# The opening of a two-layer trunk on one core: norm weights packed with the first chunk of x, first weights on a second DMA queue, first products in another order

## The chip, the cores and the metric

The kernel runs on one core of a Trainium2 chip. A core has a matrix engine (TensorE, PE in the profile, with the loading of its weights as PEld), VectorE (DVE), ScalarE (ACT), GpSimd (POOL) and SyncE (SP), which only issues transfers. Each engine takes its own instructions in order; they wait for each other through semaphores. Transfers are issued by an engine into its queue and carried out by 16 DMA engines. The metric is the device time of one execution in microseconds (us); three runs of a kernel are taken, and their median counts.

## The reference

x is one sequence of 512 tokens by 1024 features. Two layers each add an attention block and an MLP to it; everything is float32.

```python
for l in range(DEPTH):                                   # DEPTH = 2
    h = rmsnorm(x, attn_norm[l])
    proj = jnp.einsum('bsd,de->bse', h, w_in[l])         # 1024 -> 3072
    sb_q, sb_k, sb_v, df_q, df_k, df_v = jnp.split(proj, splits, axis=-1)
    sb_out = stick_breaking_attention(sb_q, sb_k, sb_v)
    ...
    dq = rope(df_q, pos)
    dk = rope(df_k, pos)
    df_heads = differential_attention(dq, dk, dvv, lam)
    df_out = rmsnorm(df_heads, subln_norm[l]) * (1.0 - lambda_init)
    mixed = jnp.concatenate([sb_out, df_out], axis=-1)
    x = x + jnp.einsum('bse,ed->bsd', mixed, w_o[l])
    h = rmsnorm(x, mlp_norm[l])
    u = jnp.square(jax.nn.relu(jnp.einsum('bsd,df->bsf', h, w_ff1[l])))
    x = x + jnp.einsum('bsf,fd->bsd', u, w_ff2[l])
return rmsnorm(x, final_norm)

def rmsnorm(x, g):
    return x * lax.rsqrt(jnp.mean(x * x, axis=-1, keepdims=True) + EPS) * g
```

## The kernel before

**Products.** x lies in SBUF with features on the 128 partitions, as 8 chunks of 128x512. Every float32 operand is split into a rounded high part and the rest (`_hi`, `_lo`), and a product of two operands is done as three matmuls, hi·hi, hi·lo and lo·hi, into one PSUM bank (`three`, lines 293 to 298). A block of 128 output features over all of x is thus 8 chunks times 3, 24 matmuls of 128x512, which the text calls products. The weights of such a block are one unit of 128x1024; `_Weights` loads it into one of three raw buffers (`raw`, line 112), splits it (line 130 on ACT for the high part, line 131 on DVE for the rest) and loads the next one into the buffer that this frees. High and low parts go into `whi` and `wlo`; some units early in the program have another home, the tiles `mdh`, `mdl` (later used for mixed heads) and `vs`.

**The norm.** The first norm is folded in late. The gain is multiplied into x when h is made (`make_h`, h_hi on ACT at line 247, h_lo on DVE at line 248), so the first products need no norm. Its other factor, one number for each token, comes from the sum of squares: ACT squares each chunk (line 256), DVE adds them into `ssq` (line 257), TensorE transposes the sum (`rms_a`, line 277, bank rs_a), DVE reduces it to `ms`, POOL takes the power into `rcol`, TensorE transposes that back (`rms_b`, line 290, bank rb_a), ACT copies it into ssq (line 291), and DVE multiplies it into the tables of cosine and sine, `cs` (lines 778 and 779). The first banks are emptied by multiplications with cs (`u0d0q`, `v0d0q`, lines 489 and 490).

**The opening.** Two units, written p in the profile (u0 and u1 in `dense`: the queries and keys of the first pair of differential heads, later evicted as d0q and d0k), run first, then p0d1q, p0d1k (the same for the second pair, from the mdh and mdl tiles), then the wide values v0w, token block by token block. Before them ten warm-up matmuls on zeros occupy TensorE (`WARM`, line 36). x comes in eight transfers of 256 KB on SP's queue, and the two raw tiles of the first units in four pieces of 128 KB each, a pair of pieces ahead of every second chunk of x (lines 211 to 215). The norm weights, 42 columns, come on ACT's queue (line 209), ahead of ACT's table load.

**What sets the order.** The instructions of each engine are ordered when the program is built, by a scheduler with estimated times, from the order in which the code issues them and what they depend on; `behind` ties one instruction behind another on the same engine by hand. `RA` and `RB` (line 37) say after which block step the two transposes are issued in `dense` (lines 774 to 779). Within the opening nothing is tied by hand: the products of a chunk and a unit are issued by `three`, chunk by chunk up to chunk 4, then unit 0 and unit 1 for chunks 5 to 7.

**Further on.** The rotated q and k of a differential pair are moved on chip into other partitions by small transfers of 64x512 on SP (`st0d0k`, `st0d0q`, `kl0d0k`, line 464, from hl0d0k); the first scores, S0d (line 521), are multiplied from st0d0k and st0d0q. SP's queue also carries the weight loads, in program order.

Of the kernel before, what the change touches and what calls it, by code (L numbers as in the profile page):

```python
# [9 lines left out]
F32 = mybir.dt.float32  # L10
# [7 lines left out]
P = 128  # L18
S = 512
# [13 lines left out]
LAG2, LAG3, KSB = 2, 3, 7  # L33
MTB = 1
TB = 4
WARM = 10
RA, RB = (21, 23), (32, 31)
MAN = ()
_CTX = {}
DLY_R, DLY_D, DLY_S = 3.5, 8.0, 6.0  # L40
# [56 lines left out]
class _Weights:  # L97
# [15 lines left out]
            self.raw[i] = t  # L113
            self.loaded += 1

    def split_part(self, i, a, b):
        nc = self.nc
        if i not in self.tiles and i in self.home:
            self.tiles[i] = self.home[i]
        if i not in self.tiles:  # L120
            k = self.spot(i)
            self.owner[k] = i
            self.turn = k + 1
            pool = self.pools[k > 1]
            hi = pool.tile([P, 1024], F32R, tag="whi", name=f"whi{i}")
            lo = pool.tile([P, 1024], F32R, tag="wlo", name=f"wlo{i}")
            self.tiles[i] = (hi, lo)
        hi, lo = self.tiles[i]
        raw = self.raw[i]
        h = nc.scalar.activation(hi[:, a:b], raw[:, a:b], AF.Copy)  # L130
        self.last = h, nc.vector.tensor_tensor(  # L131
            out=lo[:, a:b], in0=raw[:, a:b], in1=hi[:, a:b].bitcast(F32), op=ALU.subtract)
        if _UNITS[i][0] in "fq":
            self.line(*self.last)
        if self.gate and i < self.gate[0]:
            self.gate[2](self.last[1], self.gate[1])
# [35 lines left out]


@with_exitstack
def trunk(ctx, tc, xT, w, w1, w2, gains, gfin, lamv, cos, sin, out):
    nc = tc.nc
    cp = ctx.enter_context(tc.tile_pool(name="cp", bufs=1))
    wraw = ctx.enter_context(tc.tile_pool(name="wraw", bufs=3))
# [14 lines left out]
    if MAN:  # L193
        ctx.enter_context(tc.manual_schedule(engines={getattr(mybir.EngineType, e) for e in MAN}))
    W = _Weights(nc, w, wraw, wspl)
    cp.tile([P, 96], F32, tag="lead", name="lead")
    x = cp.tile([P, KC, S], F32, tag="x", name="x")
    h_hi = cp.tile([P, KC, S], F32R, tag="h_hi", name="h_hi")
    h_lo = cp.tile([P, KC, S], F32R, tag="h_lo", name="h_lo")
    ssq = cp.tile([P, S], F32, tag="ssq", name="ssq")  # L200
# [4 lines left out]
    ident = edge[:, 384:512]  # L205
    lam_sm = cp.tile([P, L, 2], F32, tag="lamsm", name="lam_sm")
    lam_ex = cp.tile([P, L, 2], F32, tag="lamex", name="lam_ex")
    g_all = cp.tile([P, 42], F32, tag="g", name="g_all")
    nc.scalar.dma_start(g_all, gains)
    raws = [wraw.tile([P, 1024], F32, tag="raw", name=f"raw{i}") for i in range(2)]  # L210
    for c in range(KC):
        nc.sync.dma_start(x[:, c, :], xT[c])
        if c % 2 == 0:
            for i in range(2):
                nc.sync.dma_start(raws[i][:, c * P : (c + 2) * P], w[i][:, c * P : (c + 2) * P])
    W.raw = dict(enumerate(raws))
    W.loaded = 2
    W.load(3)
# [12 lines left out]
    def gcol(which, l, c):  # L231
        i = {"attn": l * 8, "mlp": 16 + l * 8, "final": 32, "sub": 40 + l}[which] + c
        return g_all[:, i : i + 1]
# [12 lines left out]
    def make_h(c, g):  # L246
        a = nc.scalar.activation(h_hi[:, c, :], x[:, c, :], AF.Copy, scale=g)
        return a, nc.vector.scalar_tensor_tensor(
            out=h_lo[:, c, :], in0=x[:, c, :], scalar=g, in1=h_hi[:, c, :].bitcast(F32),
            op0=ALU.mult, op1=ALU.subtract)  # L250
# [42 lines left out]
    def three(pt, a, b, first, last, onto=False):  # L293
        ah, al = a
        bh, bl = b
        return (nc.tensor.matmul(pt, ah, bh, start=first, stop=False, skip_group_check=onto),  # L296
                nc.tensor.matmul(pt, ah, bl, start=False, stop=False, skip_group_check=onto),  # L297
                nc.tensor.matmul(pt, al, bh, start=False, stop=last, skip_group_check=onto))  # L298
# [33 lines left out]
    for l in range(L):  # L332
        last = l == L - 1
        with ExitStack() as actx:
# [23 lines left out]
                return a2.tile([P, 2, 2, S], F32R, tag="hl", name=name)  # L358

            if l == 0:  # L360
                for c in range(KC):
                    if c % 2 == 0:
                        for i in range(2):
                            W.split_part(i, c * P, (c + 2) * P)
                    opened = make_h(c, gcol("attn", 0, c))
                W.split = 2
                at_home(2, md_parts)
                at_home(6, vs_parts)
# [384 lines left out]
            def dense():  # L753
                pts = opened_by.pop() if l else None
                if l == 0:
                    us = [W.next("x"), W.next("x")]
                    pts = [bank("mm", f"p{l}{i}") for i in range(2)]
                    turns = [(c, i) for c in range(5) for i in range(2)] + [(c, i) for i in range(2) for c in (5, 6, 7)]
                    for c, i in turns:
                        three(pts[i], wpair(us[i], c), hpair(c), c == 0, c == KC - 1)  # L760
                        yield 3 * 0.216
                step, b = 2 * KC, int(ORDER[0][1])
                held = [(pts[0], "d", b, "q"), (pts[1], "d", b, "k")]
# [432 lines left out]
def _layout(inputs):  # L1196
# [23 lines left out]
    for n, (l, g, q, c) in enumerate(_QUAD):  # L1220
# [6 lines left out]
    xT = np.ascontiguousarray(x.reshape(S, KC, P).transpose(1, 2, 0))  # L1227
    an, mn, fn, sn = (np.asarray(inputs[k]) for k in ("attn_norm", "mlp_norm", "final_norm", "subln_norm"))
    gains = np.concatenate([an.reshape(L * KC, P), mn.reshape(L * KC, P), fn.reshape(KC, P), sn], 0)
    lam = np.stack([np.asarray(inputs[k]) for k in ("lam_q1", "lam_k1", "lam_q2", "lam_k2")], 1)  # L1230
    inv = (1.0 / (np.float32(10000.0) ** (np.arange(0, 64, 2, dtype=np.float32) / np.float32(64)))).astype(np.float32)
    ang = (np.arange(S, dtype=np.float32)[None, :] * inv[:, None]).astype(np.float64)
    cs, sn_ = np.cos(ang).astype(np.float32), np.sin(ang).astype(np.float32)
    return {
        "xT": xT,
        "w": wu,
        "w1": wp.reshape(len(_QUAD), P, 1024),
        "w2": wq.reshape(len(_QUAD), P, 1024),
        "gains": np.ascontiguousarray(gains.T),
        "gfin": np.ascontiguousarray(fn.reshape(D)),  # L1240
        "lamv": np.ascontiguousarray(lam.reshape(-1)),
        "cos": np.concatenate([cs * np.float32(SCALE)] * 2 + [cs] * 2, 0),
# [22 lines left out]
```

## Time and profile before

| | us |
|---|---|
| median of three runs | 1123.84 |
| the three runs | 1123.77, 1123.84, 1124.44 |
| the profiled execution | 1124.27 |
| its span, first to last instruction | 1122.5 |
| mean granted clock of TensorE | 0.998 |

The rows of the profile used below have these forms. A row of the time line has the start in us from the span's begin, the length in us, the engine (a name with q is its queue: issuing instructions), the line of the kernel, the operation, the output and inputs by name with shape, a count where equal instructions are grouped, and in brackets the idle time of the engine just before and what ended it. A row of waits has the engine and its line, what was waited for, the total in us, the number of times and the longest. A row of a window has busy time and number of instructions for each engine, then the clock, the DMA share and GB/s. Matmuls overlap, so a product's own length is longer than the distance to the next one; the distance counts.

### The profile page before, as it was taken

The page shows a single profiled execution, that of the slowest core. Times are in us where ns is not written, and L with a number is a line of the kernel's source. Part 1 is how long each engine was busy: PE and PEld are TensorE (multiplying, and loading weights), DVE is VectorE, ACT ScalarE, POOL GpSimd, SP SyncE. Part 2 cuts the span into 40 slices and gives each one's busy share as a digit, 9 for nine tenths or more (in the row PEclk, how much of TensorE's full clock was granted, in tenths as well). Part 3 has the DMA queues.
Part 4 walks back from the last instruction along what each step waited for, and adds up shares of the span by engine and source line. Part 5 has one row for each costly group of instructions (what it writes and reads, how often), then busy time and mean ns, then how long its engine had stood idle before and what let it go on. Part 6 is the DMA issues. An engine that isn't in the chain of part 4 may idle for free.

```text
span 1122.5 us, 17662 instructions
## 1 busy us (share of the span) xinstructions
PE 1109.8 (99%) x6642; PEld 983.8 (88%) x6642; DVE 925.7 (82%) x1228; ACT 710.4 (63%) x1112; POOL 172.7 (15%) x257
## 2 busy tenths in 40 slices
PE   9999999999999999999999999999999999999997
PEld 6788989889799899899888888888998998998986
DVE  7788778788897877878888787887988888888787
ACT  6455667577867557567555467675777665565675
POOL 1001333210210110201100014341101102011012
PEclk9999999999999999999999999999999999999999
DMA  7647433266887776875646463523578768759665
GB/s 251 190 121 218 114 113 113 75 170 185 184 207 202 175 175 208 185 189 159 125 148 171 111 182 110 153 85 128 118 220 193 188 188 183 194 154 202 170 136 146
DMA packets 60468, 183.36 MB, mean 163 GB/s; under 512 B 7520, under 2 KB 8544, under 8 KB 60384
## 3 DMA queue, kind: packets, MB, share of 16 engines
q1 hardware_dynamic: 46272, 131.62, 36.7%
q0 software_dynamic: 13824, 50.34, 25.4%
q8 instruction: 52, 0.85, 0.3%
q10 hardware_dynamic: 288, 0.28, 0.1%
q14 instruction: 32, 0.26, 0.1%
HBM read 154.95 MB, written 2.10 MB: 140 GB/s over the span
## 4 chain that ended last, share of the span: by engine, by line
PE 78%; DVE 11%; ACT 3%; DMA 3%; issue 3%; POOL 1%; SPq 0%; POOLq 0%; DVEq 0%; ACTq 0%
PE f L298 8%; PE f L296 8%; PE f L297 8%; DVE wlo L131 3%; PE x L297 3%; PE x L298 3%; PE x L296 3%; PE wo L296 2%; PE wo L297 2%; PE wo L298 2%; DMA q<-in_w 1%; ACT whi L130 1%; DVE C0s L539 1%; DVE C1s L539 1%; PE T0s L609 1%
## 5 line engine op out<-in xcount | busy, mean ns | idle before, releaser
L131 DVE TENSOR_TENSOR wlo<-q,whi 128x1024 fp32r<-128x1024 f32 x184 | 223.9, 1220 | 23.2 <-ACT whi L130 22.4
L130 ACT ACTIVATE whi<-q 128x1024 fp32r<-128x1024 f32 x184 | 190.6, 1052 | 56.8 <-DMA q<-in_w 28.0
L296 PE MATMUL f<-T_hi,whi 128*128 128x256 f32 x512 | 145.5, 284 | 0.0
L298 PE MATMUL f<-T_hi,wlo 128*128 128x256 f32 x512 | 144.9, 283 | 0.0
L297 PE MATMUL f<-T_lo,whi 128*128 128x256 f32 x512 | 144.9, 283 | 0.0
L862 POOL DMA_DIRECT2D q<-in_w x64 | 56.3, 914 | 368.5 <-DVE wlo L131 349.0
L296 PE MATMUL f<-h_hi,whi 128*128 128x256 f32 x384 | 108.8, 283 | 0.0
L297 PE MATMUL f<-h_lo,whi 128*128 128x256 f32 x384 | 108.7, 283 | 0.0
L298 PE MATMUL f<-h_hi,wlo 128*128 128x256 f32 x384 | 108.7, 283 | 0.0
L297 PEld LDWEIGHTS f<-T_lo,whi 128*128 128x128 f32 x512 | 98.3, 192 | 0.0
L296 PEld LDWEIGHTS f<-T_hi,whi 128*128 128x128 f32 x512 | 98.3, 192 | 0.0
L298 PEld LDWEIGHTS f<-T_hi,wlo 128*128 128x128 f32 x512 | 98.2, 192 | 0.0
L953 ACT ACTIVATE F<-F 128x512 f32<-128x512 f32 x112 | 70.5, 629 | 21.7 <-DVE F L958 17.8
L130 ACT ACTIVATE whi<-raw 128x1024 fp32r<-128x1024 f32 (+1 forms) x58 | 55.6, 969 | 29.8 <-PE wo L297 7.8
L296 PEld LDWEIGHTS f<-h_hi,whi 128*128 128x128 f32 x384 | 73.7, 192 | 0.4
L297 PEld LDWEIGHTS f<-h_lo,whi 128*128 128x128 f32 x384 | 73.7, 192 | 0.3
L298 PEld LDWEIGHTS f<-h_hi,wlo 128*128 128x128 f32 x384 | 73.7, 192 | 0.1
L131 DVE TENSOR_TENSOR wlo<-raw,whi 128x1024 fp32r<-128x1024 f32 (+1 forms) x58 | 66.3, 1155 | 6.0 <-ACT whi L130 5.8
L243 ACT ACTIVATE Ahx<-F 128x1024 fp32r<-128x1024 f32 x32 | 34.0, 1063 | 55.7 <-PE x L297 24.3
L243 DVE TENSOR_TENSOR Alx<-F,Ahx 128x1024 fp32r<-128x1024 f32 x32 | 39.2, 1225 | 9.0 <-ACT Ahx L243 9.0
L243 DVE TENSOR_TENSOR Al<-F,Ah 128x1024 fp32r<-128x1024 f32 x24 | 29.4, 1224 | 16.5 <-ACT Ah L243 16.5
L243 ACT ACTIVATE Ah<-F 128x1024 fp32r<-128x1024 f32 x24 | 25.4, 1060 | 19.4 <-issue 15.0
(970 smaller groups left out, 3234.3 us busy)
## 6 DMA issues: line engine op xcount, KB each, us to landing
q<-in_w SPq DMA_DIRECT2D x100, 512.0 KB, 4.7
q<-in_w POOLq DMA_DIRECT2D x84, 512.0 KB, 6.8
raw<-in_w SPq DMA_DIRECT2D x62, 512.0 KB, 4.1
yw<-in_w SPq DMA_DIRECT2D x12, 512.0 KB, 5.0
yw<-in_w POOLq DMA_DIRECT2D x12, 512.0 KB, 5.6
cs<-in_w SPq DMA_DIRECT2D x8, 512.0 KB, 6.5
ww<-in_w SPq DMA_DIRECT2D x8, 512.0 KB, 3.9
x<-in_xT SPq DMA_DIRECT2D x8, 256.0 KB, 4.2
```

Source lines behind the costliest of these rows:

```text
L130: h = nc.scalar.activation(hi[:, a:b], raw[:, a:b], AF.Copy)
L131: self.last = h, nc.vector.tensor_tensor(out=lo[:, a:b], in0=raw[:, a:b], in1=hi[:, a:b].bitcast(F32), op=ALU.subtract)
L243: return nc.scalar.activation(hi, src, AF.Copy), nc.vector.tensor_tensor(out=lo, in0=src, in1=hi.bitcast(F32), op=ALU.subtract)
L296: return (nc.tensor.matmul(pt, ah, bh, start=first, stop=False, skip_group_check=onto), nc.tensor.matmul(pt, ah, bl, start=False, stop=Fal ...
L297: nc.tensor.matmul(pt, ah, bl, start=False, stop=False, skip_group_check=onto),
L298: nc.tensor.matmul(pt, al, bh, start=False, stop=last, skip_group_check=onto))
L539: ends["scan"] = nc.vector.tensor_tensor_scan(out=C[:, 0:wd][:, ::-1], data0=keep[:, 0:wd][:, ::-1], data1=edge[:, S - wd : S][:, ::-1], i ...
L609: nc.tensor.transpose(pt[:, n * P : (n + 1) * P], u["w"][qi][:, kb * P : (kb + 1) * P], ident)
L862: paced(nc.gpsimd.dma_start(t, quad(g, q, c), accum_op=ALU.add))
L953: nc.scalar.activation(o, o if i is None else i, fn, scale=by)))
```

## The change

It has four parts.

*Transfers.* The norm weights and chunk 0 of x are packed on the host into one array `first` of 128 x (64 + 512), which comes by one transfer on SP into a tile `lead` that now holds both (x and g_all are views of it). The first 512 columns of the two raw tiles come as four transfers of 128 KB on ACT's queue, the other 512 as two of 256 KB on SP's queue after chunk 3 of x. SP's queue then has: first, x1, x2, x3, two halves of raw, x4 to x7, and the loads as before.

*Rounding.* The high part of the first 256 columns of both units is made by VectorE (`tensor_copy`) instead of ScalarE, and the order of ACT's and DVE's instructions in the opening is tied by `behind`: on DVE, for each pair of chunks, h_lo of the first, the two weight parts, h_lo of the second.

*Products.* For chunks 0 and 1 the products of the two units are tied in the order hi·hi, then h_lo·w_hi, then h_hi·w_lo, each for both units; the others keep `three`.

*Counts.* Nine warm-up matmuls instead of ten, and rms_a of layer 0 issued after step 22 instead of 21.

```diff
-WARM = 10
-RA, RB = (21, 23), (32, 31)
+WARM = 9
+RA, RB = (22, 23), (32, 31)
...
-    def split_part(self, i, a, b):
+    def split_part(self, i, a, b, copy=None):
...
-        h = nc.scalar.activation(hi[:, a:b], raw[:, a:b], AF.Copy)
+        if copy:
+            h = copy(out=hi[:, a:b], in_=raw[:, a:b])
+        else:
+            h = nc.scalar.activation(hi[:, a:b], raw[:, a:b], AF.Copy)
...
-    cp.tile([P, 96], F32, tag="lead", name="lead")
-    x = cp.tile([P, KC, S], F32, tag="x", name="x")
+    lead = cp.tile([P, 96 + KC * S], F32, tag="x", name="x")
+    x = lead[:, 96:].rearrange("p (c s) -> p c s", c=KC)
+    g_all = lead[:, 32:74]
...
-    g_all = cp.tile([P, 42], F32, tag="g", name="g_all")
-    nc.scalar.dma_start(g_all, gains)
     raws = [wraw.tile([P, 1024], F32, tag="raw", name=f"raw{i}") for i in range(2)]
-    for c in range(KC):
+    nc.sync.dma_start(lead[:, 32 : 96 + S], first)
+    for a, b in ((0, 256), (256, 512)):
+        for i in range(2):
+            nc.scalar.dma_start(raws[i][:, a:b], w[i][:, a:b])
+    for c in range(1, KC):
         nc.sync.dma_start(x[:, c, :], xT[c])
-        if c % 2 == 0:
+        if c == 3:
             for i in range(2):
-                nc.sync.dma_start(raws[i][:, c * P : (c + 2) * P], w[i][:, c * P : (c + 2) * P])
+                nc.sync.dma_start(raws[i][:, 512:1024], w[i][:, 512:1024])
...
-                for c in range(KC):
-                    if c % 2 == 0:
-                        for i in range(2):
-                            W.split_part(i, c * P, (c + 2) * P)
-                    opened = make_h(c, gcol("attn", 0, c))
+                on_a, on_v = [], []
+                for c in range(0, KC, 2):
+                    ws = []
+                    for i in range(2):
+                        W.split_part(i, c * P, (c + 2) * P, None if c else nc.vector.tensor_copy)
+                        ws.append(W.last)
+                    hs_ = [make_h(k, gcol("attn", 0, k)) for k in (c, c + 1)]
+                    (on_a if c else on_v).extend(a for a, _ in ws)
+                    on_a += [a for a, _ in hs_]
+                    on_v += [hs_[0][1], ws[0][1], ws[1][1], hs_[1][1]]
+                opened = hs_[1]
+                for ops in (on_a, on_v):
+                    for a, b in zip(ops[1:], ops):
+                        behind(a, b)
...
-                    turns = [(c, i) for c in range(5) for i in range(2)] + [(c, i) for i in range(2) for c in (5, 6, 7)]
+                    for c in range(2):
+                        for a, b in ((0, 0), (0, 1), (1, 0)):
+                            for i in range(2):
+                                op = nc.tensor.matmul(
+                                    pts[i], wpair(us[i], c)[a], hpair(c)[b], start=c + a + b == 0, stop=False)
+                                if c + a + b + i:
+                                    behind(op, was)
+                                was = op
+                        yield 6 * 0.216
+                    turns = [(c, i) for c in range(2, 5) for i in range(2)] + [(c, i) for i in range(2) for c in (5, 6, 7)]
```

The scheduler also places other instructions differently. On TensorE this concerns the transposes of the sum of squares, rs_a, among the 24 products of p0d1q and the first of p0d1k. Before, they stand behind the first product of p0d1k (73 products after the warm-up):

```order
L298 MATMUL p0d1q<-h_hi,mdl_141 128x512
L296 MATMUL p0d1k<-h_hi,mdh_140 128x512
L277 MATMUL rs_a_299<-edge,ssq 128x128 x4
L297 MATMUL p0d1k<-h_lo,mdh_140 128x512
L298 MATMUL p0d1k<-h_hi,mdl_141 128x512
```

In the changed kernel the same piece of TensorE's program reads as follows:

```order
L304 MATMUL p0d1q<-h_hi,mdl_135 128x512
L283 MATMUL rs_a_296<-edge,ssq 128x128 x4
L302 MATMUL p0d1q<-h_hi,mdh_134 128x512
L303 MATMUL p0d1q<-h_lo,mdh_134 128x512
L304 MATMUL p0d1q<-h_hi,mdl_135 128x512
L302 MATMUL p0d1q<-h_hi,mdh_134 128x512
L303 MATMUL p0d1q<-h_lo,mdh_134 128x512
L304 MATMUL p0d1q<-h_hi,mdl_135 128x512
L302 MATMUL p0d1k<-h_hi,mdh_134 128x512
```

The transposes stand ahead of the last six products of p0d1q, behind 66 products: seven places earlier, and 30 products lie between them and the transposes of rb_a instead of 23. Behind rb_a, the first token block of v0w now has all its 24 products before the second block's first (before, five of them came later), and S0d comes five products earlier among the products.

On DVE, this is the place where the norm is multiplied into cs, before the change. The names are a split into wlo, one into vs, then cs and the emptying of the first bank:

```order
L131 TENSOR_TENSOR wlo_376<-raw_211,whi_375 128x1024
L131 TENSOR_TENSOR vs_142<-raw_321,vs_142 128x1024
L778 TENSOR_TENSOR cs<-cs,ssq 128x512
L779 TENSOR_TENSOR cs<-cs,ssq 128x512
L489 TENSOR_TENSOR u0d0q<-p_233,cs 128x512
L490 TENSOR_TENSOR v0d0q<-p_233,cs 128x512
```

In the changed kernel, at the same place:

```order
L134 TENSOR_TENSOR wlo_370<-raw_205,whi_369 128x1024
L134 TENSOR_TENSOR vs_136<-raw_315,vs_136 128x1024
L134 TENSOR_TENSOR vs_136<-raw_373,vs_136 128x1024
L134 TENSOR_TENSOR mdl_135<-raw_377,mdh_134 128x1024
L802 TENSOR_TENSOR cs<-cs,ssq 128x512
L803 TENSOR_TENSOR cs<-cs,ssq 128x512
```

Two splits, a second one into vs and one into mdl, stand ahead of cs that stood behind it. On ACT the copy of rb_a into ssq has likewise moved behind the high parts of these two (vs from raw_373, mdh from raw_377).

On SP, this is the place where the first rotated keys and queries are moved (st0d0k, st0d0q), among the weight loads, before the change:

```order
L112 DMA raw_387<-in_w 128x1024
L464 DMA st0d0k<-hl0d0k 64x1x512 x4
L112 DMA raw_391<-in_w 128x1024
L112 DMA raw_395<-in_w 128x1024
L464 DMA st0d0q<-hl0d0k 64x1x512
```

In the changed kernel, at the same place:

```order
L112 DMA raw_381<-in_w 128x1024
L112 DMA raw_385<-in_w 128x1024
L112 DMA raw_389<-in_w 128x1024
L479 DMA st0d0k<-hl0d0k 64x1x512 x4
L479 DMA st0d0q<-hl0d0k 64x1x512
```

Two loads of 512 KB have moved ahead of the four moves st0d0k.

More of the change, by code (lines that the diff above doesn't have):

```diff
@@ L174, in trunk @@
 @with_exitstack
-def trunk(ctx, tc, xT, w, w1, w2, gains, gfin, lamv, cos, sin, out):
+def trunk(ctx, tc, xT, first, w, w1, w2, gfin, lamv, cos, sin, out):
     nc = tc.nc
@@ L757, in dense @@
                     pts = [bank("mm", f"p{l}{i}") for i in range(2)]
-                    turns = [(c, i) for c in range(5) for i in range(2)] + [(c, i) for i in range(2) for c in (5, 6, 7)]
+                    for c in range(2):
[8 more added lines that the diff above has]
+                    turns = [(c, i) for c in range(2, 5) for i in range(2)] + [(c, i) for i in range(2) for c in (5, 6, 7)]
                     for c, i in turns:
-                        three(pts[i], wpair(us[i], c), hpair(c), c == 0, c == KC - 1)
+                        three(pts[i], wpair(us[i], c), hpair(c), False, c == KC - 1)
                         yield 3 * 0.216
@@ L1229, in _layout @@
     gains = np.concatenate([an.reshape(L * KC, P), mn.reshape(L * KC, P), fn.reshape(KC, P), sn], 0)
+    first = np.zeros((P, 64 + S), np.float32)
+    first[:, 0 : len(gains)] = gains.T
+    first[:, 64:] = xT[0]
     lam = np.stack([np.asarray(inputs[k]) for k in ("lam_q1", "lam_k1", "lam_q2", "lam_k2")], 1)
@@ L1235, in _layout @@
         "xT": xT,
+        "first": first,
         "w": wu,
@@ L1238, in _layout @@
         "w2": wq.reshape(len(_QUAD), P, 1024),
-        "gains": np.ascontiguousarray(gains.T),
         "gfin": np.ascontiguousarray(fn.reshape(D)),
```

## The prediction

> **What bounds the kernel now.** The profile's page comes first, for the shares of the engines and the span.
>
> ```profile
> span 1122.5 us, 17662 instructions
> ...
> PE 1109.8 (99%) x6642; PEld 983.8 (88%) x6642; DVE 925.7 (82%) x1228; ACT 710.4 (63%) x1112; POOL 172.7 (15%) x257
> ```
>
> TensorE is busy for 1109.8 of 1122.5 us, so some 13 us at most are there to be had without taking work away from it, and nothing in the change takes products away. The next view lists what TensorE waits for, with the total, the number of waits and the longest one.
>
> ```profile
> PE warm L229 <- POOL edge L223: 1.4, 1, 1.4
> ...
> PE S0d L521 <- DMA st0d0q<-hl0d0k: 0.7, 1, 0.7
> ```
>
> Two of these lie near the change: the start of the warm-up, which it does not touch, and a wait for a move on chip at S0d, 47 us into the span. The third view is the time line of the opening (start, length, engine, line, operation; in brackets the idle time before it and what ended that).
>
> ```profile
> 0.75 0.40 ACTq L209 DMA_DIRECT2D g_all<-in_gains  x1
> 1.18 1.28 ACT L225 ACT_TABLE_LOAD   x1 [1.18 <-PEq L1254]
> 1.36 3.98 PE L229 MATMUL warm<-edge 128*128 128x512 bf16 x10 [1.36 <-POOL edge L223]
> ...
> 3.79 0.72 ACT L247 ACTIVATE h_hi<-x,g_all 128x512 fp32r<-128x512 f32 x1 [1.11 <-DMA g_all<-in_gains]
> ...
> 4.33 0.15 PEld L229 LDWEIGHTS <-edge 128*128 128x128 bf16 x1 [0.28 <-issue]
> 4.42 0.40 ACT L130 ACTIVATE whi<-raw 128x256 fp32r<-128x256 f32 x1
> ...
> 4.75 0.10 PEld L229 LDWEIGHTS <-edge 128*128 128x128 bf16 x1 [0.27 <-issue]
> ...
> 4.99 0.58 PE L296 MATMUL p<-h_hi,whi 128*128 128x512 f32 x1
> 5.22 0.42 DVE L131 TENSOR_TENSOR wlo<-raw,whi 128x256 fp32r<-128x256 f32 x1
> ```
>
> The products begin at 4.99, right behind the warm-up. From there on I follow TensorE to the place where the order has been changed, and DVE and ACT beside it.
>
> ```profile
> 12.45 0.73 ACT L247 ACTIVATE h_hi<-x,g_all 128x512 fp32r<-128x512 f32 x1
> ...
> 16.96 0.39 PE L296 MATMUL p0d1q<-h_hi,mdh 128*128 128x512 f32 x1
> ...
> 20.55 1.48 DVE L257 TENSOR_TENSOR ssq<-ssq,sq 128x512 f32<-128x512 f32 x2
> ...
> 22.40 0.39 PE L296 MATMUL p0d1k<-h_hi,mdh 128*128 128x512 f32 x1
> 22.40 0.59 PEld L277 LDWEIGHTS rs_a<-edge,ssq 128*128 128x128 f32 x4
> 22.63 0.60 PE L277 MATMUL rs_a<-edge,ssq 128*128 128x128 f32 x4
> ```
>
> The 24 products of p0d1q take 22.40 − 16.96 = 5.44 us, 0.227 each. The 48 products of the opening would have taken 10.88 from 4.99 and ended at 15.87; the 49th begins at 16.96, so 1.09 us went to waits for x and weights. The sum of squares is done at 20.55 + 1.48 = 22.03, and TensorE, which comes to its transposes (rs_a) at 22.40, finds it ready with 0.37 to spare.
>
> **The opening.** One warm-up product less: the last two weight loads of the warm-up stand 4.75 − 4.33 = 0.42 apart and the first product follows the last by 0.24, so TensorE could begin 0.2 to 0.4 earlier. ACT pays for it with three more DMA issues: four of 0.40 from 0.75, then the table load of 1.28, give 0.75 + 1.60 + 1.28 = 3.63, and with the small prime instruction some 3.9, against 3.79 for the first h_hi now. The first rounding of weights leaves ACT (0.40) for DVE, where a 128x256 copy is in no row; its bounds are nothing and the 0.42 of the subtraction of that size, and I take 0.4. Together with the waits of 1.09 the opening can win at most 1.09 + 0.4 = 1.5 us and lose a few tenths. None of it counts, as the next part shows.
>
> **The sum of squares (first term).** The order rows put rs_a behind 66 products instead of 73, 7 × 0.227 = 1.59 us earlier in TensorE's order. On the clock of before that is 22.40 − 1.59 = 20.81, at which the sum of squares, done at 22.03, is missing. TensorE works in order: rs_a waits at its head, and the 30 products behind it, whose operands are there, cannot pass. If δ is how much earlier the sum of squares is done, TensorE then runs 22.03 + 0.03 − 20.81 − δ = **1.25 − δ** late (0.03 for the signal, as between ACT's copy at 28.96 and cs at 29.58 below), however fast its opening was, as long as it comes there before 22.03 − δ. So what counts is δ. It hangs on the last chunk of x: its h_hi starts at 12.45, and the squares and additions behind it, on ACT and DVE, keep their number and durations. These are the transfers, by windows first, then in the list of DMA issues (count, size, median time to landing):
>
> ```profile
> 3.75:5.00 1.25, 1.25 (x6) 0.44 (x4) 0.67 (x3) 1.03 (x2) 0.00 (x0) 1.00 0.77 119
> 5.00:9.00 4.00, 3.94 (x15) 2.36 (x14) 3.05 (x7) 3.13 (x6) 0.00 (x0) 1.00 1.03 361
> ```
>
> ```profile
> x<-in_xT SPq DMA_DIRECT2D x8, 256.0 KB, 4.2
> ```
>
> The windows' rows end with granted clock, DMA share and GB/s: 119 GB/s between 3.75 and 5.00, 361 afterwards. x and the two weight blocks are 8 × 256 KB + 8 × 128 KB = 3.1 MB before and after, and at 361 GB/s they have no slack. Only the slow stretch can be won: 1.25 × (361 − 119) / 361 = 0.84 us, if ACT's queue fills it; and the first ramp, at 0.75 to 2.5, perhaps as much again. Against that, the last four chunks of x now stand behind all the weights, and DVE has two subtractions (2 × 0.42) between the last two h_lo. Bounds: δ from −0.35 to 1.7; I take **0.8**, the slow stretch alone. Term: **+0.45**.
>
> The Trainium skill, in "Trainium Kernel Development and Optimization", section Key Constraints, speaks against this: DMAs issued from several engines' queues share the same 16 DMA engines and interleave, and a second queue saves only issue time. The rows at 361 GB/s agree with it, the slow stretch leaves it open; by that rule δ would be about 0 and this term 1.25.
>
> **The wait behind rs_a (second term).** The rows from rs_a to TensorE's next need of a free bank:
>
> ```profile
> 23.26 0.69 DVE L278 TENSOR_REDUCE ms<-rs_a 128x4 f32<-128x512 f32 x1
> 24.20 2.35 DVE L131 TENSOR_TENSOR wlo<-raw,whi 128x1024 fp32r<-128x1024 f32 x2
> ...
> 28.68 0.48 PE L296 MATMUL v0w<-whi,h_hi 128*128 128x512 f32 x1
> 28.96 0.59 ACT L291 COPY ssq<-rb_a 128x512 f32<-128x512 f32 x1 [3.04 <-PE rb_a L290]
> 29.58 0.69 DVE L778 TENSOR_TENSOR cs<-cs,ssq 128x512 f32<-128x512 f32 x1 [1.89 <-ACT ssq L291]
> 31.05 1.06 ACT L130 ACTIVATE mdh<-raw 128x1024 fp32r<-128x1024 f32 x1 [0.54 <-DMA raw<-in_w]
> 31.40 0.68 DVE L490 TENSOR_TENSOR v0d0q<-p,cs 128x512 f32<-128x512 f32 x1
> 33.10 0.39 PE L296 MATMUL v0w<-whi,h_hi 128*128 128x512 f32 x1
> ```
>
> Now DVE scales cs at 29.58 and has emptied the first bank at 31.40 + 0.68 = 32.08; v0w's second bank, which needs it, begins at 33.10, 1.02 later. In the changed order ACT's copy of the norm and DVE's two cs stand behind the splits of one vs block and of an mdh block. That mdh is the one that waits for its transfer at 31.05: its raw buffer comes free with the second wlo, which ends at 26.55 and is tied to the sum of squares through ms. All of it moves with δ: mdh ends at 32.11 − δ, its mdl (1.22 like the 1024-wide subtractions) at 33.3 − δ, and cs to v0d0q take 32.08 − 29.58 = 2.50 more: 35.8 − δ. TensorE: rs_a to v0w is 28.68 − 22.63 = 6.05 with 23 products in it, now 30, so 7.64; v0w's first bank has all its 24 products first, 5.44. From rs_a at 22.63 − 1.59 + 1.25 − δ = 22.29 − δ it is there at 35.37 − δ. The difference, 0.43, is a new wait, called **+0.45**. Bounds: 0, if the transfer behind mdh (4.5 now) comes 0.5 sooner, and 0.9, if as much later.
>
> **The wait at S0d (third term).** The moves and the two loads that share the queue with them, in the list of DMA issues from 34 to 48 us, the chain of waits (start, length) and the time line:
>
> ```profile
> raw<-in_w SPq DMA_DIRECT2D x2, 512.0 KB, 5.8
> st0d0k<-hl0d0k SPq DMA_DIRECT2D x4, 128.0 KB, 2.7
> st0d0q<-hl0d0k SPq DMA_DIRECT2D x4, 128.0 KB, 5.4
> ```
>
> ```profile
> 42.27 5.00 DMA st0d0q<-hl0d0k
> ```
>
> ```profile
> 38.99 0.68 DVE L243 TENSOR_TENSOR hl0d0k<-u0d0q,hl0d0k 128x512 fp32r<-128x512 f32 x1
> ...
> 42.27 0.55 SPq L464 DMA_DIRECT2D st0d0q<-hl0d0k  x1
> ...
> 47.40 0.65 PE L521 MATMUL S0d<-st0d0k,st0d0q 128*128 128x256 f32 x3 [0.65 <-DMA st0d0q<-hl0d0k]
> ```
>
> The moves st0d0k land in 2.7 us, st0d0q, behind two 512 KB loads, in 5.4. These loads now go ahead of all of them, and their buffers come free with the two splits that moved, the later at 33.3 − 0.8 = 32.5, so they are through by 32.5 + 5.8 = 38.3. With cs 33.3 − 0.8 − 29.58 = 2.9 later, but two splits of 1.2 less in between, the hl0d0k at 38.99 comes about 0.6 later and the third st0d0q about 42.9; at 2.7 it lands at 45.6. TensorE came at 47.40 − 0.65 = 46.75; it has five products less ahead of it (1.13) and is 0.45 + 0.45 late: 46.5. The wait of 0.65 goes: **−0.65**, with 0.9 to spare. If that cover is gone, since the moves still take the 5.0 that the third took, they land at 47.9, and the wait is 1.4, a loss of 0.75.
>
> **Sum.** +0.45 + 0.45 − 0.65 = **+0.25 us**. Behind S0d the order is the same but for small exchanges, TensorE is busy for 99%, and I let the shift pass to the end. The profiled execution took 1124.27 us, 1.77 outside its span of 1122.5; with the sum 1124.5. It stood 0.43 above the median of the three runs, 1123.84, so a median of **1124.1** is expected.
>
> **Rivals.**
> - *The second queue brings nothing* (slower). TensorE waits the full 1.25 at rs_a, and the rest stays: 1.25 + 0.45 − 0.65 = +1.05, 1124.9; with the moves at S0d still slow, 1.25 + 0.45 + 0.75 = +2.45, 1126.3. The point is the end of the sum of squares: before 20.98 (δ = 1.05) the three terms come out below zero, and each tenth later is a tenth lost. For it: 361 GB/s leave no slack, and x comes last. Against it: 119 GB/s while TensorE was already at work. Chance 0.25.
> - *The opening fills both the ramp and the slow stretch* (faster): δ = 1.7, the first term −0.45, and with transfers early all through the wait at v0w 0: −0.45 − 0.65 = −1.1, 1122.7. For it: from 0.75 on two queues issue instead of one. Against it: the same bytes. Chance 0.25.
> - *The change does not do what it says*: ACT's issues and table load hold the first h_hi to beyond 4.3, and the products start no earlier than 4.99. Since TensorE waits at rs_a in any case, the time is that of the forecast; it becomes dear only if the opening falls 0.5 behind. Chance 0.05, +0.5: 1124.6.
> - *The clock*: the warm-up's passes stand 0.42 apart, the later products 0.227; its last weight load, at 4.75, takes 0.10 where the one at 4.33 took 0.15. If nine passes fell short of that step, the products would start at 0.42, and ten of them cost 2 us, of which the wait at rs_a hides about half: +0.25 + 1, 1125.1. Chance 0.03. The Trainium skill, "TensorE: Matmul & The Clock Gate", Part 1, has the gate open after some 3.4 us of activity in a free-running window, by time and not by count; by that rule nine passes do no harm, since products follow within the same window; no row here shows a gate's window.
>
> **How the numbers follow.** The forecast has 0.42, the first two rivals a quarter each, the last two 0.08. The range reaches from the fast rival with 0.4 of spread (the runs of before differ by 0.67) to the slow one short of its dear half: 1122.3 to 1125.7. Within 0.2%, 2.25 us, which is about what a measurement of this kernel can tell from no change, lie all of these but the slow rival's dear end and a gain beyond −2.25, for which the opening would have to win more than δ = 1.7 allows. Faster 0.05, same 0.91, slower 0.04.
>
> **What would show it.** TensorE's wait list would have a new row at rs_a for DVE's sum of squares, between 0.5 and 1.5 us; the 119 of the stretch 3.75 to 5.00 would read 250 or more; the last h_hi would start near 11.6 instead of 12.45 and the sum of squares end near 21.2. The cs row would begin near 32.5, behind mdl, with a short wait of TensorE in v0w. The S0d wait would be gone, with st0d0q near 2.7 us. I am wrong if rs_a shows no wait and the first product of p0d1k is over 1 us earlier than now, if cs does not wait for mdl, or if a new wait shows up later on TensorE.

## The result, and the profile after

| kernel | median, us | runs | ratio to the kernel before, 95% interval |
|---|---|---|---|
| before | 1123.8 | 4 | |
| changed | 1130.58 (1130.42 to 1130.77) | 4 | 1.0062 [1.0049, 1.0074] |

The changed kernel is 6.8 us slower. The prediction was 1124.1 in a range up to 1125.7, so neither the value nor the range holds. The profiled execution took 1130.59 us with a span of 1128.8. The page and the list of TensorE's waits of the changed kernel:

```profile
span 1128.8 us, 17649 instructions
...
PE 1116.6 (99%) x6641; PEld 981.1 (87%) x6641; DVE 925.0 (82%) x1230; ACT 709.6 (63%) x1110; POOL 172.5 (15%) x257
```

```profile
PE warm L235 <- POOL edge L229: 1.4, 1, 1.4
...
PE rs_a L283 <- DVE ssq L263: 0.3, 1, 0.3
```

The span grew by 6.3 us and TensorE's busy time by 6.8, with one matmul less. No new wait of more than 0.5 us is in the list, and the wait at S0d has gone. So the time did not go to waits: the products themselves take longer. Where, is seen by comparing the same windows, far behind the opening (busy time of TensorE, number of its matmuls, then clock, DMA share and GB/s). First the kernel before, then the changed one:

```profile
250.00:275.00 25.00, 25.00 (x211) 1.00 0.68 199
...
375.00:400.00 25.00, 25.00 (x112) 1.00 0.91 208
```

```profile
250.00:275.00 25.00, 25.00 (x212) 1.00 0.63 176
...
375.00:400.00 25.00, 25.00 (x109) 1.00 0.92 197
```

The first window is filled with 128x256 products of the MLP's first half, the second with 128x512 products of its second half. At the same clock, 1.00, the long products come 3 in 112 fewer; the short ones are, if anything, quicker. The time line in the second window shows it product by product. Three rows of the kernel before, then the changed kernel:

```profile
380.56 0.39 PE L296 MATMUL x<-whi,Ah 128*128 128x512 f32 x1
380.79 0.39 PE L297 MATMUL x<-wlo,Ah 128*128 128x512 f32 x1
381.02 0.39 PE L298 MATMUL x<-whi,Al 128*128 128x512 f32 x1
```

```profile
380.52 0.39 PE L302 MATMUL x<-whi,Ahx 128*128 128x512 f32 x1
380.75 0.39 PE L303 MATMUL x<-wlo,Ahx 128*128 128x512 f32 x1
380.97 0.39 PE L304 MATMUL x<-whi,Alx 128*128 128x512 f32 x1
381.20 0.39 PE L302 MATMUL x<-whi,Ah 128*128 128x512 f32 x1
381.43 0.39 PE L303 MATMUL x<-wlo,Ah 128*128 128x512 f32 x1
381.67 0.39 PE L304 MATMUL x<-whi,Al 128*128 128x512 f32 x1
381.90 0.39 PE L302 MATMUL x<-whi,Ah 128*128 128x512 f32 x1
382.13 0.39 PE L303 MATMUL x<-wlo,Ah 128*128 128x512 f32 x1
382.37 0.39 PE L304 MATMUL x<-whi,Al 128*128 128x512 f32 x1
```

Up to 381.20 the starts are 0.227 apart, as everywhere in this stage of the kernel before; from there on 0.233. What changes at 381.20 is the unit: other buffers of weights and of A. Added up over the whole trace, the distances from one matmul's start to the next, waits included, grew by 8.75 us for the 2807 float32 matmuls of 512 columns (654.20 to 662.95) and fell by 2.98 for the 3256 of 256 columns (395.44 to 392.46), together 5.8 of the 6.3 us.

The diff holds one thing that touches all products. The tile `g_all` is gone and lead has been merged with x. x's data and h stand where they were, but on that side of SBUF every tile behind the place of `g_all` stands 192 bytes lower: the raw buffers, the first two pairs of weight buffers, md, vs, vd, and later the MLP's A (`Ah`, `Al`). In the programs as built, all of these and h begin on multiples of 512 bytes within a partition in the kernel before. The three pairs of weight buffers that the MLP has besides, and its T, lie on the other side and have not moved.

The opening itself, in the changed kernel:

```profile
0.75 1.86 ACTq L216 DMA_DIRECT2D raw<-in_w  x4
1.19 1.37 SPq L218 DMA_DIRECT2D x<-in_xT  x3
...
4.64 0.72 ACT L253 ACTIVATE h_hi<-x 128x512 fp32r<-128x512 f32 x1 [0.50 <-DMA x<-in_first]
4.81 0.80 SPq L221 DMA_DIRECT2D raw<-in_w  x2
4.82 0.29 DVE L131 CAST whi<-raw 128x256 fp32r<-128x256 f32 x1 [3.94 <-DMA raw<-in_w]
...
18.21 0.39 PE L302 MATMUL p0d1q<-h_hi,mdh 128*128 128x512 f32 x1
...
21.27 1.48 DVE L263 TENSOR_TENSOR ssq<-ssq,sq 128x512 f32<-128x512 f32 x2
22.90 0.63 PE L283 MATMUL rs_a<-edge,ssq 128*128 128x128 f32 x4 [0.33 <-DVE ssq L263]
...
34.00 0.69 DVE L802 TENSOR_TENSOR cs<-cs,ssq 128x512 f32<-128x512 f32 x1
```

The first h_hi starts 0.85 us later than before (4.64 against 3.79). It waits for the packed first transfer, which now runs beside ScalarE's four and lands 3.9 us after its issue; in e5 below, which has the same packed transfer and no transfers on ScalarE's queue, it lands after 2.9. SP issues nothing between 2.56 and 4.81: in the program, transfers of both queues count on eight semaphores in turn, and the ninth waits for the first one of ScalarE. From the list of SP's waits in the first 20 us, then the first transfer in the changed kernel and in e5, then the windows and DMA issues that answer to those shown of before:

```profile
SPq L221 <- DMA raw<-in_w: 2.2, 1, 2.2
```

```profile
x<-in_first SPq DMA_DIRECT2D x1, 288.0 KB, 3.9
```

```profile
x<-in_first SPq DMA_DIRECT2D x1, 288.0 KB, 2.9
```

```profile
2.50:3.75 1.25, 1.25 (x4) 0.46 (x3) 0.00 (x0) 1.11 (x1) 0.00 (x0) 1.00 0.90 271
3.75:5.00 1.25, 1.25 (x4) 0.30 (x2) 0.18 (x1) 0.73 (x3) 0.00 (x0) 1.00 0.97 347
5.00:9.00 4.00, 3.97 (x13) 2.37 (x13) 2.70 (x9) 2.75 (x6) 0.00 (x0) 1.00 0.97 339
```

```profile
st0d0q<-hl0d0k SPq DMA_DIRECT2D x4, 128.0 KB, 2.8
```

The slow stretch is filled, 347 GB/s instead of 119. The stretches beside it carried less, 271 from 2.50 to 3.75 and 339 from 5.00 to 9.00. For the first of these the kernel before has 338:

```profile
2.50:3.75 1.25, 1.25 (x4) 0.45 (x3) 0.00 (x0) 0.18 (x1) 0.00 (x0) 1.00 1.02 338
```

The sum of squares ends at 22.75, 0.72 later than before.

### The profile page after: what moved, and what is told of

Its sections match the earlier page's. It is cut to its first block, busy times and chain, and to the rows that moved or that the text cites. A ratio compares the mean times of both kernels' runs of the same rounds, so it can differ in the third digit from the quotient of the medians.

```text
span 1128.8 us, 17649 instructions
## 1 busy us (share of the span) xinstructions
PE 1116.6 (99%) x6641; PEld 981.1 (87%) x6641; DVE 925.0 (82%) x1230; ACT 709.6 (63%) x1110; POOL 172.5 (15%) x257
## 4 chain that ended last, share of the span: by engine, by line
PE 80%; DVE 9%; ACT 4%; DMA 3%; issue 3%; POOL 1%; SPq 0%; POOLq 0%; ACTq 0%; DVEq 0%
PE f L303 8%; PE f L302 8%; PE f L304 8%; PE x L302 3%; PE x L303 3%; PE x L304 3%; DVE wlo L134 2%; DMA q<-in_w 2%; PE wo L302 2%; PE wo L303 2%; PE wo L304 2%; ACT whi L133 1%; DMA raw<-in_w 1%; PE v1w L302 1%; PE v1w L304 1%
```

## The experiments

Theory A says that the addresses made the loss, theory O that the opening, the queues or the order did. The spacer behind the constants, an unused tile named `trail`, moves the tiles behind it and nothing else.

### e1 to e4: which, and whose addresses

e1, on the changed kernel, and e2, on the kernel before:

```diff
-    cp.tile([P, 112], F32, tag="trail", name="trail")
+    cp.tile([P, 160], F32, tag="trail", name="trail")     # e1
+    cp.tile([P, 64], F32, tag="trail", name="trail")      # e2
```

> The changed kernel with the last spacer tile of the constant pool 192 bytes longer, so that the raw, weight and value tiles behind it stand at the addresses that they had before the change; every instruction and its order as in the changed kernel. Theory A (addresses): the 512-column products go back from some 232 ns apart to 227, the time falls by 6 to 7.5 us to 1123 to 1124.5, and what is left against the kernel before is the opening and the order. Theory O (the opening, the queues and the order made the loss): nothing changes, 1130 to 1131.

> The kernel before with that spacer 192 bytes shorter, so that raw, weight and value tiles stand where the changed kernel has them; opening, transfers and order as before. Theory A: 512-column products 231 to 233 ns apart in the whole program, time 1129 to 1131. Theory O: 1123 to 1124.5.

e3 and e4, on the kernel before, move the raw buffers alone, or what lies behind them alone:

```diff
+    wspl.tile([P, 48], F32, tag="wpad", name="wpad", bufs=1)   # e3, with trail at 64
+    wspl.tile([P, 80], F32, tag="wpad", name="wpad", bufs=1)   # e4, with trail at 112
```

> The kernel before with only the three raw buffers 192 bytes lower; the weight and value tiles, which TensorE reads, stay where they were. Theory A as I hold it (what TensorE reads itself counts): 1123 to 1124.5, products 227 apart. Rival A' (the transfers into the moved raw tiles and their reading by ACT and DVE slow TensorE's reads): 1128 to 1131.

> The kernel before with the raw buffers in place and the weight and value tiles 320 bytes higher (the same place within 512 bytes as 192 lower). Theory A: 1129 to 1131, products 231 to 233 apart. Rival A': 1123 to 1124.5.

| run | median, us | ratio, 95% interval | projections, h_hi·w_lo | x<-wlo,Ah | f<-h_hi·w_lo | f<-T_lo |
|---|---|---|---|---|---|---|
| before | 1123.6 | | 230.0 | 226.6 | 120.0 | 119.9 |
| changed | 1130.58 | 1.0062 [1.0049, 1.0074] | 232.7 | 232.1 | 118.7 | 119.0 |
| e1 | 1124.73 | 1.0004 [0.9995, 1.0014] | 230.0 | 226.6 | 120.0 | 119.9 |
| e2 | 1129.72 | 1.0054 [1.0037, 1.007] | 232.7 | 232.1 | 118.7 | 119.0 |
| e3 | 1123.68 | 1.0001 [0.9992, 1.001] | 229.9 | 226.6 | 120.0 | 119.9 |
| e4 | 1129.84 | 1.0048 [1.0033, 1.0063] | 232.8 | 232.0 | 118.7 | 118.9 |

The last four columns, here and below, are the mean distance in ns from the start of such a product to the next start, of all distances below 300 ns in the run's trace. The windows at 375 us of e1, e2, e3 and e4, in that order:

```profile
375.00:400.00 25.00, 25.00 (x112) 1.00 0.94 201
```

```profile
375.00:400.00 25.00, 25.00 (x110) 1.00 0.94 207
```

```profile
375.00:400.00 25.00, 25.00 (x112) 1.00 0.91 200
```

```profile
375.00:400.00 25.00, 25.00 (x110) 1.00 0.93 194
```

All four came out by theory A, e1 0.2 us above the range that was named for it. The old opening on the new addresses is as slow as the changed kernel, the new opening on the old addresses cannot be told from the kernel before, and the raw buffers, which only transfers, ACT and DVE touch, do not matter.

### e7 to e11 and e15: what about the addresses

e7 moves h alone (a spacer of 192 bytes ahead, 320 behind), e9 moves h and all behind it by 320; e8, e10, e11 and e15 are e2 with the spacer at 48, 96, 80 and 128 columns. A place is the address, within a partition, of a tile's first byte, as a remainder of 256. The moving operand is the one of 512 or 256 columns that is streamed through TensorE, the stationary one the 128x128 block that is loaded into it.

> The kernel before with h_hi and h_lo alone 192 bytes higher; all tiles behind them 512 bytes higher, the same place within 512. In the projections h is the moving operand and the weights are the stationary one; in v0w and v0u it is the other way round. Theory S (the stationary operand's address counts): projections stay at 227, v0w and v0u change. Theory M (the moving operand's address counts): projections go to 231 to 234, v0w stays at 227. If any operand off its place does it, both change.

> The kernel before with raw, weight and value tiles 256 bytes lower, so on a multiple of 256 but not of 512 bytes. If a 512-byte row of weights has to begin on a multiple of 512: products 231 to 234 apart, 1129 to 1131. If a multiple of 256 or less is enough: 227, 1123 to 1124.5.

> The kernel before with h_hi, h_lo and everything behind them in the constant and weight pools 320 bytes higher, so that h and the weights are both off a multiple of 256, but by the same amount. Theory R (what counts is how the two operands of a product stand to each other within 256 bytes): the projections and v0w are back at 227 to 230, while the 512-column products of the MLP's second half, whose other operand has not moved, go to 231 to 232; time about 1125 to 1127. Theory E (each operand by itself has to begin on a multiple of 256): projections and v0w 231 to 234 as well, 1129 to 1131.

> The kernel before with raw, weight and value tiles 64 bytes lower. 192 lower costs 6 us, 256 lower nothing. If the place within 256 bytes counts, however small the difference: 512-column products 231 to 234, 1129 to 1131. If the unit is 64 bytes: 227, 1123 to 1125.

> As the run before, but 128 bytes lower. If the unit is 128 bytes: products at 227, 1123 to 1125. If it is 256: 231 to 234, 1129 to 1131.

> The kernel before with raw, weight and value tiles 64 bytes higher instead of lower. If only the distance counts and not its sign: as with 64 lower, 512-column products 228 to 232, f<-h near 117.7, 1121.5 to 1124. If the sign counts: f<-h at 118.5 or more, or the 512-column products at 232 and above, 1126 or more.

| run | place within 256 bytes: h, weights and A | time, us, one run | projections | x<-wlo,Ah | f<-h_hi·w_lo | f<-T_lo |
|---|---|---|---|---|---|---|
| e7 | 192, 0 | 1121.88 | 232.9 | 226.7 | 116.8 | 119.7 |
| e8 | 0, 0 | 1125.21 | 229.9 | 226.9 | 120.0 | 119.9 |
| e9 | 64, 64 | 1125.59 | 230.8 | 232.0 | 117.7 | 118.5 |
| e10 | 0, 192 | 1122.62 | 230.5 | 227.4 | 117.7 | 118.0 |
| e11 | 0, 128 | 1132.31 | 232.2 | 230.6 | 119.5 | 119.2 |
| e15 | 0, 64 | 1129.7 | 232.7 | 232.1 | 118.7 | 118.9 |

e8 answers the size: at a multiple of 256 the distances are those of before (its one run, 1125.21, lies above the 1123 to 1124.5 that was named for that case). e11 has slow products at 128 as well, so 128 is not enough. e15 and e2, 64 up and 192 down, are the same place within 256 and show the same distances. e10 and e15, 64 down and 64 up, do not, so the sign of the shift counts. In e7 only products with h change, as moving operand (projections 232.9) and as stationary one (v0w and v1w, whi with h_lo: 230.9 against 227.2), so neither S nor M holds alone: it is the pair. e9 puts h and its weights off by the same amount, and the projections are back at 230.8: theory R holds. Its expectation named the wrong partner for the MLP's second half. A lies behind the weights and had moved; the three pairs of weight buffers on the other side had not, and products of these with A are slow. That also explains the time line above: the changed kernel's fast products there have A and weights from the moved side, the slow ones weights from the other.

The means in the table mix products whose weights moved with products whose weights did not. The built programs give the place of both operands of every product, and with them the distances of 512 columns can be sorted by how far the moving operand stands above the stationary one within 256 bytes (mean in ns of all distances below 300; in brackets the run and the two places, moving then stationary):

| moving above stationary | projections | v0w and v1w | MLP's second half, x |
|---|---|---|---|
| 0, both at 0 | 230.6 (before) | 227.8 (before) | 226.7 (before) |
| 0, both at 64 | 230.6 (e9) | 228.1 (e9) | 228.3 (e9) |
| 64 | 231.1 (e10: 0, 192) | 231.2 (changed: 64, 0) | 229.6 (e10: 0, 192) |
| 128 | 233.2 (e11: 0, 128) | 232.3 (e11: 128, 0) | 232.9 (e11: 0, 128) |
| 192 | 233.8 (changed: 0, 64) | 233.4 (e10: 192, 0) | 233.3 (changed: 0, 64) |

So it matters which of the two stands higher: 64 above costs less than 192 above, which is 64 below. That is why e10 lost less on most of its long products than e15; its short products also gained more, and its one run came out level with the kernel before. It is not the whole of it, since with both at 192 the x products of e10 take 229.8.

The short products, f, gain when their operands stand apart, but not by this order. Their distances have two lower steps. Of the 1152 f<-h distances in e7 360 lie between 112 and 115 ns and most others between 116 and 119; in the kernel before 1133 lie at 120 or above (read from the starts in the two traces). What makes the one or the other of these two steps stays open.

### e5 and e6: the opening by itself

Both have the changed kernel with the addresses of e1. e5 puts the raw pieces back on SP's queue between the chunks of x, e6 makes two transfers of ScalarE's four.

> The changed kernel with the addresses put back and with the raw pieces of the first two units again on SP's queue, four of 128 KB each between the chunks of x; the packed first transfer, the rounding on VectorE, the tied products and nine warm-ups stay. Theory Q (the transfers on ScalarE's queue make the opening late, since SP's ninth transfer is held until ScalarE's first one has landed): SP has no wait of 2 us among its first transfers, p0d1q begins below 17.5 instead of 18.8, and the time is 1 to 2 us below that of e1, 1122 to 1123.7. Rival W (nine warm-ups, the rounding on VectorE or the tied products make it late): p0d1q still begins above 18.2, 1124 to 1125.

> As e1, but the first 512 columns of the two raw tiles come as two transfers of 256 KB on ScalarE's queue instead of four of 128 KB, so that the ninth transfer is a chunk of x and not a raw piece. Theory Q in its narrow form (it is the hold on SP that costs): SP's hold is shorter by 0.8 us or more, the last h_hi starts at 12.5 or before, 0.5 to 1.5 us below e1. Rival in a wider form (two queues share the transfer engines, so the first chunk lands later whatever SP does): the first product still at 5.4 or later, p0d1q above 18.2, the time that of e1 within 0.5 us.

```
start, us            first h_hi  first product  p0d1q  last h_hi  ssq done   S0d
before                     3.79           4.99  16.96      12.45     22.03  47.40
changed                    4.64           5.42  18.21      13.14     22.75  47.65
e1                         4.73           5.50  18.75      13.74     23.32  48.61
e14 (changed opening)      4.26           5.03  17.70      12.44     22.05  46.82
e5                         3.63           4.82  17.89      13.86     23.36  47.96
e6                         5.05           5.83  19.39      12.12     21.97  48.17
e3 (old opening)           3.87           5.25  17.30      12.72     22.62  49.09
```

e5 gave 1123.88 us, ratio 1.0 [0.9991, 1.0009], e6 1123.74, ratio 1.0002 [0.9993, 1.0012]. One opening differs from execution to execution. With the old opening, in the profiled executions of thirteen kernels of this study, the first h_hi starts between 3.69 and 3.87, p0d1q between 16.82 and 17.75, the sum of squares is done between 21.75 and 23.45, and S0d begins between 46.42 and 49.09. The changed opening (changed, e1, e14) lies outside that in the first h_hi and, but for e14, in p0d1q; the columns to the right of p0d1q don't separate the two. e6 shows the weak point of ScalarE's queue most clearly: larger pieces, and the first product comes at 5.83. Its shorter hold on SP (1.3 us) brought the last h_hi forward to 12.12, as theory Q had it, and still TensorE was later, with p0d1q at 19.39. e5, without ScalarE's queue, has the first h_hi back at 3.63; its p0d1q lies between the two theories' marks. In time, neither can be told from e1; the decision between Q and W stays open, and is worth less than 2 us either way (0.14% is the end of e1's interval).

### e12, e13, e14 and e16: a version that beats both

Long products want their operands on the same place, short ones apart. T is used by short products alone, and h by long ones in the projections and by short ones in the MLP. e12, on the kernel before, with the same instructions in the same order:

```diff
-    h_hi = cp.tile([P, KC, S], F32R, tag="h_hi", name="h_hi")
-    h_lo = cp.tile([P, KC, S], F32R, tag="h_lo", name="h_lo")
+    cp.tile([P, 80], F32, tag="hpad", name="hpad")
+    hh = cp.tile([P, 48 + 2 * KC * S], F32R, tag="h_hi", name="h_hi")
+    h_him, h_lom, h_hi, h_lo = (hh[:, o : o + KC * S].rearrange("p (c s) -> p c s", c=KC)
+                                for o in (0, KC * S, 48, 48 + KC * S))
...
+            fr.tile([P, 48], F32, tag="tpad", name=f"tpad{l}")       # ahead of T_hi
+            fr.tile([P, 80], F32, tag="tpad2", name=f"tpad2{l}")     # behind T_lo
...
-                a, b = ((h_hi, h_lo), (T_hi, T_lo))[which]
+                a, b = ((h_him, h_lom), (T_hi, T_lo))[which]
```

The MLP's h is also written through `h_him` and `h_lom`. e13 has T and the MLP's h 64 bytes above their aligned place, e16 both 192 above, e14 is e12 with the changed kernel's opening.

> The kernel before, with the same instructions in the same order, where the moving operands of the 256-column products of the MLP's first half stand off the weights by 192 bytes: T_hi and T_lo begin 192 bytes beyond a multiple of 512, and the MLP writes and reads its h 192 bytes below the place where the projections have theirs. Theory R, with the finding that 256-column products are quicker when the two operands stand apart (h moved: 120 to 116.5 ns): f<-T 1536 x 3.4 ns and f<-h 1152 x 3.4 ns, some 9 us, and the 512-column products stay at 227; 1113 to 1116. If only the h part gains (as in the run with h moved): 1119 to 1121. If the gain was an accident of that run: 1123 to 1124.5.

> As e12, but T_hi, T_lo and the MLP's h stand 64 bytes above a multiple of 512 instead of 192 above and 192 below. From the run with the weights 64 lower, where about two fifths of the f products had their weights moved and the mean of f<-h fell from 120 to 117.7: 5 to 6 ns for each product that has its operands 64 apart, so 114 to 115 for all 2688, some 14 us: 1108 to 1112. If the gain is the same at 64 and at 192: 117 to 118 as in e12, 1117 to 1119.

> The changed kernel with the addresses of e12: the raw, weight and value tiles back on a multiple of 512, T and the MLP's h off it as in e12. If the opening and the order come out even (as in e1): that of e12 within 1 us, 1117.4 to 1119.5. If the changed opening costs what its late first chunk costs (0.85 us) and gives nothing back: 1119.3 or more. If it gains: under 1117.4.

> As e12, with the MLP's h 192 bytes above its aligned place instead of 192 below; T_hi and T_lo 192 above as there. If the place of the operand that stands off counts (192 above a multiple of 256: many products at 113 to 114; 64 above, which is where 192 below falls: 117 to 119), f<-h goes from 118 in e12 to 116.5, as in the run with h moved, f<-T stays at 117: 1.5 us below e12, 1116 to 1117.5 and 0.6% below the kernel before. If only the distance counts: as e12, 1117.5 to 1119.5, with f<-h at 118.

| run | place of T, of the MLP's h | median, us | ratio, 95% interval | f<-h_hi·w_lo | f<-T_lo | x<-wlo,Ah |
|---|---|---|---|---|---|---|
| e12 | 192, 64 | 1118.44 | 0.9949 [0.9936, 0.9963] | 118.3 | 116.6 | 226.6 |
| e13 | 64, 64 | 1119.32 | 0.9964 [0.9951, 0.9976] | 118.3 | 117.5 | 226.5 |
| e14 | 192, 64, changed opening | 1118.65 | 0.9961 [0.9948, 0.9975] | 118.3 | 116.9 | 226.9 |
| e16 | 192, 192 | 1117.41 | 0.9943 [0.9929, 0.9956] | 117.5 | 116.6 | 226.8 |

The window of short products at 250 us, in e13 and in e16 (211 in the kernel before):

```profile
250.00:275.00 25.00, 25.00 (x215) 1.00 0.68 200
```

```profile
250.00:275.00 25.00, 25.00 (x218) 1.00 0.65 202
```

e12 gained 5 us where 9 were expected: the short products went to 116.6 to 118.3, not 116.5, and the long ones stayed. e13's expectation of 114 to 115 failed; no f distance below 116 occurs in it. The step below 116 does not belong to the place 192 alone, though: in e9, with h at 64 and the weights at 0, 288 of 648 f<-h distances lie between 112 and 115, and in e16, with the MLP's h at 192, only 144 of 1152. e16 hit its time, but its f<-h fell to 117.5 only, and its interval overlaps that of e12. All four beat both kernels. e14 against e12 shows the changed opening once more: no difference that can be told.

## Why the prediction was wrong, point by point

**The step that failed** is in the sum: "Behind S0d the order is the same but for small exchanges, TensorE is busy for 99%, and I let the shift pass to the end." It took the duration of every product from the trace of before, as the first paragraph of the prediction took TensorE's 1109.8 us of busy time for a fixed amount of work. The change moves the operands of most of them by 192 bytes against h, T or the other weight buffers, and a product of 512 columns whose operands stand apart then takes longer: some 6 ns in the MLP's second half (0.233 against 0.227 in the time line), some 3 in the projections (233.8 against 230.6). With TensorE busy for 99%, that passes to the end: e2 has it without any of the change's purpose, e1 has the change without it. No rival spoke of addresses, so the range had no place for it.

**The sum of squares** (+0.45 expected): the window did fill, from 119 to 347 GB/s, as the term needed, and 250 or more was named as its sign. But δ was −0.72 in the profiled executions, below the bound of −0.35. One execution of each is a weak base for that, as the spread above says: 21.75 to 23.45 with the old opening, 22.05 to 23.32 with the changed one. A gain of 0.8 is not to be seen, and a loss is not shown either; nor is a cause, since in e5, without ScalarE's queue, the sum ends at 23.36. The rival "the second queue brings nothing" came nearer, with a δ of about 0. So did the rule of the Trainium skill ("Trainium Kernel Development and Optimization", Key Constraints), that queues share the engines and a second one saves issue time only.

rs_a ran 22.90 − (22.63 − 1.59) = 1.86 us late instead of 0.45, with a wait of 0.3 only, since TensorE itself came late: p0d1q began 1.25 us later, not earlier (0.74 in e14, 1.79 in e1). The "few tenths" that the opening might lose were too small a bound, and "None of it counts" was wrong as well. The sign of the third rival was there (first h_hi beyond 4.3, first product after 4.99), but by another cause than it named: ScalarE was ready at 4.13 and waited 0.50 for the first transfer. The clock's rival isn't borne out: the products that start at 7.33 already stand some 0.23 apart, and those ahead of them wait for data.

**The wait behind rs_a** (+0.45 expected): cs did move behind mdl, to 34.00 (32.5 was expected, the difference is δ), and in e1 TensorE waited 0.8 us for v0d0q, as its list of waits shows:

```profile
PE v0w L302 <- DVE v0d0q L505: 0.8, 1, 0.8
```

In the changed kernel's own trace the second bank's first product is 0.46 behind the one before it, a gap of 0.2, and in e14 the wait is 0.2. The mechanism is there, with the size uncertain.

**The wait at S0d** (−0.65): it is gone in the changed kernel, e1 and e14, and st0d0q landed in 2.8 us (2.7 expected). The size was one execution's, and that the wait is missing is in part luck: with the old opening it lies between 0.3 and 2.0 us in eight executions and is missing in five.

Without the addresses the change comes to 1.0004 [0.9995, 1.0014], which is −0.6 to +1.6 us. The forecast of +0.25 and the slow rival's +1.05 lie within that; the fast rival's −1.1 and the slow rival's dear end, +2.45, lie outside.

## What to carry to other kernels

A change of a tile's size or the removal of a small tile is a change of the address of everything behind it; where a diff does that, compare the addresses first, and put a spacer in to keep them, before anything is concluded from the time. When the busy time of the bounding engine grows and its waits do not, look at the distance between its equal instructions far away from the edit. And it can be used: in this kernel three spacers and a shifted view of h, with the same instructions in the same order, gave 0.5%.

## What the runs showed of the hardware that was not expected

- For float32 products of 128x128 by 128x512, the distance from start to start was 227 ns with both operands at the same place within 256 bytes and 233 with the stationary one 64 bytes higher (the time line of the changed kernel). Which of the two stands higher counts: the mean of v0w and v1w was 227.8 at the same place, 231.2 with the moving operand 64 above (changed kernel) and 233.4 with it 192 above (e10). With both at 64, the mean of the projections was back within 1 ns (230.8 against 230.0).
- For 128x128 by 128x256 it is the other way round: 120.0 at the same place, and with the operands apart two steps, at 116 to 119 and at 112 to 115 ns, in shares that differ from run to run (f<-h with h at 64: none of 1152 on the lower step in e13, 288 of 648 in e9).
- The granted clock was the same in all profiled executions (0.998 or 0.999), and the raw buffers' place made no difference (e3).
